# A diffusion step on one core: descriptor memory doubled, y tiles in the shared buffers, two dot tiles moved into the first network

## The chip, the core and the metric

The kernel runs on one core of one Trainium2 chip. The core has TensorE (PE in the profile; PEld is its weight load), VectorE (DVE), ScalarE (ACT), GpSimd (POOL) and SyncE (SP). POOL and SP issue DMA transfers, each on a queue of its own, and 16 DMA engines move the bytes for both. The metric is the time of one execution in microseconds of device time; lower is better.

## The reference

One step of a diffusion backbone with two layers, on 512 latent tokens and 128 context tokens, with 1024 features. Every sub-layer has the same frame: the input is normalised and modulated by a shift and a scale, goes through the sub-layer, and is added back to the residual with a gate.

```
m = silu(cvec) @ mod_w[i] + mod_b[i]          # six vectors of 1024 per layer and condition
h = rmsnorm(x, g) * (1 + scale) + shift
x = x + gate * mixer(h)                       # layer 0: SSD scan; layer 1: differential attention
x = x + gate2 * conv_ffn(h2)                  # h2: x normalised and modulated again

def conv_ffn(h, up_w, conv_w, conv_b, down_w):
    u = dwconv(h @ up_w, conv_w, conv_b)      # 1024 -> 2 x 2816, width 3 along the tokens
    a, v = jnp.split(u, 2, axis=-1)
    return (jax.nn.silu(a) * v) @ down_w      # 2816 -> 1024
```

The layer-0 modulation is needed at once. That of layer 1, a 6144 x 1024 matrix times two conditioning vectors, is needed only from attention on, so the kernel computes it bit by bit beside other work. These are the "dots".

## The kernel before

Features lie on the 128 partitions and the 640 tokens along the free axis, so a residual is eight tiles `x` of 128 x 640. Every matmul is made of three: operands are split into a high and a low part of a rounded format, and hi*hi, hi*lo and lo*hi are added up. Weights come through `raw` buffers by SP (`prefetch`, line 166); `cast` makes the high part on ACT (`whi`, line 103) and the low part (`wlo`) on DVE. For part of the up weights (`self.summed`) the low part is made without DVE: ACT writes minus the high part into `wlo`, and POOL issues a transfer that reads the weights from memory again and adds them to it (line 204). POOL does such accumulating transfers in two more places: the low part of the network's middle tiles (`ml<-cv`, line 724), and the sum of a down projection (`xd<-y`, line 357).

A network (`ffn`) runs over 22 pairs of hidden tiles. In the first network the first six pairs are plain products; from then on `pair8` does the pair with seven products of sums of quarter matrices, made on DVE (tiles `s`). `SUB` cuts the pairs at 4, 8, 12 and 16. After each cut (one pair into the next part) `project_out` multiplies the middle tiles by their part of the down weights, for eight output tiles: ACT scales each by its gate into a tile `y`, and POOL adds y to the residual, which lies in memory as `xd` during the network. The fifth part adds into the residual in SBUF after `restore` has loaded it.

The dots are the generator `mod_rest`. For each of 48 tiles it loads 128 x 1024 weights into one of two `mw` buffers (SP, line 667) and makes two reductions on DVE (line 674), one for each condition. `DOTS = 3, 34, 48` says where: tiles 0 to 2 before the first network, 3 to 33 in it, 34 to 47 in attention. A hook that TensorE's loops call counts steps ("ticks"); between two reductions the generator waits `self.gap` of them. In the first network a plain pair has 16 ticks and the gap is 3; a seven-product pair has 14 and the gap 10; a projection of eight tiles has 32, with a gap of 4 in the first and 5 in the next three. In attention the gap is 6. What is left of the dots is drained after the last pair of the network, and in attention before the output projection; only then is the memory of the weights and conditions given back and the residual reloaded.

Buffers have tags. `t` has 4 buffers (line of `tmp`), `f` has `NF = 11`, for raw up products (`uraw`), sums `s`, and others. In the first network the even y lie in `t`, the odd ones in a tag `y` with 2 buffers of the network's own pool; in the second all eight lie in `y` with 3. Two of the last three norm tiles that are made while the first network starts (`late`) lie in `y` as well, the third in `f`. The order of each engine's instructions is set by the planner of the framework from the program's order and its own estimate of when operands come free; a few are given high priority. POOL issues in order: a transfer that waits holds all behind it.

The program reserves `dynamic_dma_scratch_size` bytes of every partition, at address 0 of SBUF, for the descriptors of the transfers that POOL issues.

Of the kernel before, what the change touches and what calls it, by code (L numbers as in the profile page):

```python
# [40 lines left out]
RAW = 4  # L41
NS = 4
S0 = 6, 4
DOTS = 3, 34, 48
TH = T // 2
ATT_SPLIT = 6
NF = 11
# [3 lines left out]
class Step:  # L51
# [643 lines left out]
    def ffn(self, l, h, nextnorm, pool):  # L695
        nc = self.nc
# [46 lines left out]
        def operands(out, tp):  # L743

            B = [[[tuple(cut(t, j) for t in h[ns * k + i]) for i in range(ns)] for j in range(2)] for k in range(2)]
            Ts = [[], [], [], []]
            late = []
            for i in range(ns):
                f1, f2 = self.tmp("f1"), self.tmp("f2")
                for f, k in ((f1, i), (f2, ns + i)):  # L750
                    self.tt(f, h[k][0].bitcast(F32), h[k][1].bitcast(F32), ALU.add)
                    yield 1
                t12, t43 = self.slot("f", "t12", bufs=NF), self.slot("f", "t43", bufs=NF)
                self.tt(cut(t12, 0), cut(f1, 1), cut(f1, 0), ALU.subtract)
                self.tt(cut(t12, 1), cut(f2, 1), cut(t12, 0), ALU.subtract)
                self.tt(cut(t43, 0), cut(f2, 0), cut(t12, 1), ALU.subtract)
                self.tt(cut(t43, 1), cut(f2, 1), cut(f1, 1), ALU.subtract)
                yield 2
                hi, lo = (tp.tile([P, 3 * TH], F32R, tag=f"T{nm}{i}", name=f"T{nm}{i}", bufs=1) for nm in "hl")
                x4 = tuple(cut(t, 1) for t in h[i])  # L760
                late.append((x4, cut(t43, 0)))
                parts = (slice(0, T), t12), (slice(T, T + TH), cut(t43, 1))
                for o, x in parts:
                    self.act(hi[:, o], x, AF.Copy)
                    self.tt(lo[:, o], x, hi[:, o].bitcast(F32), ALU.subtract)
                    yield 1
                for j in range(3):
                    Ts[j].append((cut(hi, j), cut(lo, j)))
                Ts[3].append(x4)
                yield 2  # L770
            rest = [[tuple(cut(t, j) for t in h[k]) for k in range(2 * ns, KT)] for j in range(2)]
            out.extend((B, Ts, rest, late))
# [58 lines left out]
        def pair(p, more):  # L831
            if p >= S0[l]:
                if p == S0[l]:
                    self.drain(self.seven)
                    finish_operands()
                return pair8(p, more)
            ua = copy_out(self.next_tile(h, "up"))
            epilogue(p, ua, copy_out(self.next_tile(h, "up")))

        self.start_tiles(h)  # L840
        done = 0
# [6 lines left out]
        with self.tc.tile_pool(name=f"sums{l}", bufs=1, side="right", reuse_waits="tile") as tp:  # L848
            self.seven = self.add(operands(sevens, tp), 1)
            for s, (k0, k1) in enumerate(SUB):  # L850
                while done < min(k1 + 1, FT):
                    if not l and done == 3:
                        junk = lambda: self.slot("sq", "junk", BF16, cols=1024, bufs=1)
                        self.modtask = self.add(self.mod_rest(1, *DOTS[:2], self.cb, self.mod_row, junk), 1)
                    self.gap, self.rest = 3 if done < S0[0] else 10, 0
                    pair(done, done + 1 < min(k1 + 1, FT))
                    done += 1
                if s < len(SUB) - 1:
                    self.gap = 5 if s else 4
                    if self.modtask:  # L860
                        self.modtask[1] = self.ticks + 1
                    self.project_out(mid, range(k0, k1), self.gate(l, 1),
                                     to=lambda i: self.slot("y", "y", bufs=3 if l else 2, pool=pool) if l or i % 2
                                     else self.tmp("y"))
        if self.modtask:
            self.drain(self.modtask)
            self.modtask = None
# [271 lines left out]
    def ssd(self, h, dtps, nextnorm, pool):  # L1139
# [62 lines left out]
        self.gap, self.rest = 4, 3  # L1202
        early = self.add(self.mod_rest(1, 0, DOTS[0], self.cond_rows(row), row, junk), 8)
        self.project_last(hy, range(8), self.gate(0, 0), nextnorm, save=True, before=[early])
# [201 lines left out]
    def heads(self, h, nextnorm, pool):  # L1406
# [9 lines left out]
        self.gap, self.rest = 6, 0  # L1416
        dots = self.add(self.mod_rest(1, *DOTS[1:], self.cb, self.mod_row, junk), 10)
        for hd in range(8):
# [38 lines left out]
    def weight_units(self):  # L1457
# [9 lines left out]
        def ffn(l):  # L1467
# [13 lines left out]
            return out  # L1481

        u = [(*x, None, None) for x in u] + ffn(0)
        v, u = u, []
        for hd in range(8):
# [5 lines left out]
              for i in range(0, KT - 3, per) for j in (min(i + per, KT - 3),)]  # L1491
        u += [(a["w_ao"][i], D) for i in range(KT - 3, KT)]
        return v + [(*x, None, None) for x in u] + ffn(1)

    def run(self):
        tc, nc, a = self.tc, self.nc, self.a
        self.units = self.weight_units()
        name = lambda u: self.units[u][0] is not None and self.units[u][0].name
        up = [u for u in range(len(self.units)) if name(u) == a["w_up"].name]
        after = {u for u in up if name(u - 1) and name(u - 1) != a["w_up"].name}  # L1500
        half = len(up) // 2
        self.summed = (set(up) - set(up[:5]) - set(up[half:half + 5]) - after)
        self.x = []

        def norm(l, s, h):
            def mk(hf):
                if hf == "A":
                    h.extend(self.new_h(f"h{l}{s}"))
                return self.norm_task(hf, self.gs[l][s], self.shift(l, s), h)
            return mk  # L1510

        hs = [[] for _ in range(4)]
        psd = lambda: tc.tile_pool(name="psd", bufs=3, space=PSUM, reuse_waits="tile")
        psb = lambda: tc.tile_pool(name="psb", bufs=6, space=PSUM, reuse_waits="tile")
        self.open_x()
        scond = ExitStack()
        sp = scond.enter_context(tc.tile_pool(name="scond", bufs=1, reuse_waits="tile"))
        with psd() as self.psd:
            with tc.tile_pool(name="first", bufs=1, reuse_waits="tile") as pool, tc.manual_schedule():
                self.silu_cond(sp)  # L1520
                dtps = self.first_tiles(hs[0], pool)
            with (tc.tile_pool(name="sconst", bufs=1, reuse_waits="tile") as cp,
                  tc.tile_pool(name="ssd", bufs=1, reuse_waits="tile") as pool):
                self.ssd_consts(cp)
                self.ssd(hs[0], dtps, norm(0, 1, hs[1]), pool)
        scond.close()
        with psb() as self.psb, tc.tile_pool(name="ffn0", bufs=1, reuse_waits="tile") as pool:
            self.px = pool
            y = lambda: self.slot("y", "nty", bufs=2, pool=pool)
            self.late = [y, y, lambda: self.slot("f", "ntl", bufs=NF)]  # L1530
            self.ffn(0, hs[1], norm(1, 0, hs[2]), pool)
            self.px = None
        self.psb = None
        self.deep = 1
        with psd() as self.psd:
            self.attention(hs[2], norm(1, 1, hs[3]))
        with psb() as self.psb, tc.tile_pool(name="ffn1", bufs=1, reuse_waits="tile") as pool:
            self.px = pool
            self.ffn(1, hs[3], self.final_task, pool)
            for t in reversed(list(self.tasks)):  # L1540
                self.drain(t)
        self.xctx.close()
# [99 lines left out]
```

## Time and profile before

| | us |
|---|---|
| median of three runs (lowest, highest) | 1868.93 (1862.59, 1873.59) |
| the profiled execution's own time | 1865.18 |
| its span, first to last instruction | 1863.4 |
| first SSD mixer and what stands ahead | 0 to 566 |
| first network | 566 to 1050 |
| attention and its output projection | 1050 to 1400 |
| second network and final norm | 1400 to 1863 |

Rows of the timeline give the start, the time taken, engine, line, operation, output and inputs, and in brackets how long the engine had been idle and what the profile names as the end of that idle time. Rows of waits give the total, the number and the longest. Rows by stage give for each engine the busy time and the number of instructions, then the granted clock of TensorE, the share of the 16 DMA engines that was busy, and GB/s. A busy share above 1 comes from packets that overlap. A wait is named after the releaser that the profile can see; where POOL waits inside its own descriptor code, the name can be of an unrelated instruction.

### The profile page before, as it was taken

Reading aid. Unit: us, or ns where it says so; the run is one execution under the profiler, and the core shown is the slowest. Engines: PE = TensorE matmul, PEld = TensorE weight load, DVE = VectorE, ACT = ScalarE, POOL = GpSimd, SP = SyncE. Lnnn points to the kernel's source line nnn. Section 1 sums busy time; section 2 is a strip of 40 time slices with the busy share of each in tenths; the row PEclk is TensorE's granted clock in tenths of the full one; section 3 lists DMA queues with packets and bytes.
Section 4 is the critical chain, followed back from the end, with each engine's and each line's share of the span. In section 5 each row is a group of like instructions: output and inputs, shape, how many; then the busy total and the mean of one; then the engine's idle time right before and its main releaser. Section 6 shows DMA issues by size and latency. Waiting matters only on the chain. (4 is left out here: it accounts for less than half of the span.)

```text
span 1863.4 us, 33793 instructions
## 1 busy us (share of the span) xinstructions
PE 1786.0 (96%) x12914; PEld 1687.5 (91%) x12914; DVE 1463.6 (79%) x2907; ACT 1169.8 (63%) x2329; POOL 154.4 (8%) x180
## 2 busy tenths in 40 slices
PE   7999999999999989899989989999999999999997
PEld 5899999999899989898989988888889999999996
DVE  6699999999768867778776788888968856758584
ACT  3489687878337555676564555666636766767661
POOL 0000000000001111221210000000000121222210
PEclk9999999999999999999999999999999999999998
DMA  9835344446647686877866222222334588787871
GB/s 341 275 113 150 96 148 107 138 134 205 205 158 178 179 232 161 199 196 184 225 151 217 86 85 80 82 87 80 102 126 110 113 171 175 155 183 152 175 194 57
DMA packets 116990, 289.13 MB, mean 155 GB/s; under 512 B 13422, under 2 KB 20186, under 8 KB 116828
## 3 DMA queue, kind: packets, MB, share of 16 engines
q1 hardware_dynamic: 90908, 223.92, 36.9%
q0 software_dynamic: 25344, 62.53, 19.8%
q8 instruction: 101, 1.65, 0.4%
q10 hardware_dynamic: 576, 0.52, 0.1%
q14 instruction: 61, 0.50, 0.1%
HBM read 238.36 MB, written 34.80 MB: 147 GB/s over the span
## 5 line engine op out<-in xcount | busy, mean ns | idle before, releaser
L103 ACT ACTIVATE whi<-raw 128x1024 fp32r<-128x1024 f32 (+2 forms) x259 | 226.2, 873 | 183.2 <-PE po L112 110.6
L109 DVE TENSOR_TENSOR wlo<-raw,whi 128x1024 fp32r<-128x1024 f32 (+3 forms) x188 | 188.4, 1006 | 41.1 <-ACT whi L103 40.5
L112 PE MATMUL po<-ml,whi 128*128 128x256 f32 (+1 forms) x704 | 165.8, 309 | 2.4 <-DMA ml<-cv 2.4
L204 POOL DMA_DIRECT2D wlo<-in_w_up x70 | 62.1, 887 | 1254.9 <-DVE ca L106 590.7
L112 PE MATMUL po<-mh,whi 128*128 128x256 f32 (+1 forms) x704 | 165.7, 309 | 0.2 <-ACT mh L103 0.2
L112 PE MATMUL po<-mh,wlo 128*128 128x256 f32 (+1 forms) x704 | 165.3, 309 | 0.0
L109 DVE TENSOR_TENSOR wlo<-s,whi 128x512 fp32r<-128x512 f32 x136 | 92.0, 688 | 60.6 <-ACT whi L103 60.2
L112 PE MATMUL up<-h01h,wlo 128*128 128x320 f32 (+2 forms) x400 | 114.6, 316 | 18.2 <-DMA wlo<-in_w_up 18.2
L103 ACT ACTIVATE whi<-s 128x512 fp32r<-128x512 f32 x136 | 84.4, 629 | 74.9 <-DVE s L109 55.9
L112 PE MATMUL up<-Th,whi 128*128 128x320 f32 x408 | 127.9, 313 | 3.1 <-ACT uraw L103 3.1
L112 PEld LDWEIGHTS po<-ml,whi 128*128 128x128 f32 x704 | 127.7, 188 | 3.2 <-DMA ml<-cv 3.2
L112 PEld LDWEIGHTS po<-mh,whi 128*128 128x128 f32 x704 | 127.6, 188 | 0.7 <-ACT mh L103 0.4
L112 PEld LDWEIGHTS po<-mh,wlo 128*128 128x128 f32 x704 | 127.9, 188 | 0.1
L112 PE MATMUL up<-Th,wlo 128*128 128x320 f32 x408 | 127.4, 312 | 0.0
L112 PE MATMUL up<-Tl,whi 128*128 128x320 f32 x408 | 127.3, 312 | 0.0
L106 DVE SCALAR_TENSOR_TENSOR cv<-uraw,fcw,cv 128x511 f32<-128x511 f32 (+1 forms) x176 | 85.7, 547 | 37.5 <-ACT cv L103 37.4
L112 PE MATMUL up<-h01l,whi 128*128 128x320 f32 (+2 forms) x400 | 113.3, 313 | 0.0
L112 PE MATMUL up<-h01h,whi 128*128 128x320 f32 (+2 forms) x400 | 113.3, 313 | 0.0
L112 PE MATMUL up<-h11h,wlo 128*128 128x320 f32 (+1 forms) x368 | 107.3, 309 | 3.0 <-DMA wlo<-in_w_up 3.0
L112 PE MATMUL up<-h11l,whi 128*128 128x320 f32 (+1 forms) x368 | 107.0, 308 | 0.0
L112 PE MATMUL up<-h11h,whi 128*128 128x320 f32 (+1 forms) x368 | 107.0, 308 | 0.0
L106 DVE SCALAR_TENSOR_TENSOR ca<-uraw,fcw,ca 128x511 f32<-128x511 f32 (+1 forms) x176 | 86.8, 547 | 10.0 <-ACT ca L103 8.1
(531 smaller groups left out, 5387.2 us busy)
## 6 DMA issues: line engine op xcount, KB each, us to landing
raw<-in_w_up SPq DMA_DIRECT2D x88, 512.0 KB, 4.1
mw<-in_modT SPq DMA_DIRECT2D x45, 512.0 KB, 6.9
raw<-in_w_in SPq DMA_DIRECT2D x40, 512.0 KB, 6.0
rb<-rowd SPq DMA_DIRECT2D x40, 512.0 KB, 5.7
xd<-y POOLq DMA_DIRECT2D x64, 320.0 KB, 7.2
wlo<-in_w_up POOLq DMA_DIRECT2D x36, 512.0 KB, 6.5
raw<-in_w_dn SPq DMA_DIRECT2D x64, 256.0 KB, 2.9
ml<-cv POOLq DMA_DIRECT2D x42, 320.0 KB, 4.1
```

Source lines behind the costliest of these rows:

```text
L103: return self.nc.scalar.activation(out, in_, func, **k)
L106: return self.nc.vector.scalar_tensor_tensor(out, in0, s, in1, op0, op1)
L109: return self.nc.vector.tensor_tensor(out, a, b, op)
L112: self.last = self.nc.tensor.matmul(out, lhsT, rhs, start=start, stop=stop, skip_group_check=more)
L204: self.nc.gpsimd.dma_start(lo[:, c], self.units[u][0][:, c], accum_op=ALU.add)
```

## The change

Three things in one. The descriptor memory goes from 1024 to 2048 bytes of a partition. The tag `y` goes from the first network: odd y and the late norm tiles use `f`, and the second network keeps its three `y` buffers. Tiles 34 and 35 of the dots go from attention into the first network, where the gap falls from 10 to 9 ticks in seven-product pairs and from 5 to 4 in the second to fourth projection. No arithmetic changes.

```diff
-DOTS = 3, 34, 48
+DOTS = 3, 36, 48
...
-                    self.gap, self.rest = 3 if done < S0[0] else 10, 0
+                    self.gap, self.rest = 3 if done < S0[0] else 9, 0
...
-                    self.gap = 5 if s else 4
+                    self.gap = 4
...
-                                     to=lambda i: self.slot("y", "y", bufs=3 if l else 2, pool=pool) if l or i % 2
-                                     else self.tmp("y"))
+                                     to=lambda i: self.slot("y", "y", bufs=3, pool=pool) if l
+                                     else self.slot("f", "y", bufs=NF) if i % 2 else self.tmp("y"))
...
-            y = lambda: self.slot("y", "nty", bufs=2, pool=pool)
-            self.late = [y, y, lambda: self.slot("f", "ntl", bufs=NF)]
+            self.late = [lambda: self.slot("f", "ntl", bufs=NF)] * 3
...
-    nc = bacc.Bacc("TRN2", target_bir_lowering=False, num_devices=1, dynamic_dma_scratch_size=1024)
+    nc = bacc.Bacc("TRN2", target_bir_lowering=False, num_devices=1, dynamic_dma_scratch_size=2048)
```

## The prediction

> **What bounds the kernel now.** Read the head of the page, then the busy times by stage, then what TensorE waits for in the stage that idles most, and only then the queues behind that wait.
>
> ```profile
> span 1863.4 us, 33793 instructions
> PE 1786.0 (96%) x12914; PEld 1687.5 (91%) x12914; DVE 1463.6 (79%) x2907; ACT 1169.8 (63%) x2329; POOL 154.4 (8%) x180
> ```
>
> TensorE is busy 1786.0 of 1863.4 us, and the change alters no matmul. All it can win or lose is idle time of PE, 77 us, and time at a lower clock. Busy times of the first network from its seven-product pairs on, of attention and of the second network:
>
> ```profile
> 680.00:1000.00 320.00, 297.07 (x1956) 294.06 (x1955) 243.40 (x446) 201.51 (x367) 58.64 (x67) 0.97 0.77 190
> 1060.00:1330.00 270.00, 254.50 (x1775) 225.05 (x1773) 235.73 (x481) 166.87 (x351) 0.00 (x0) 0.99 0.26 82
> 1440.00:1800.00 360.00, 357.04 (x2435) 356.10 (x2435) 244.73 (x439) 249.54 (x458) 74.42 (x85) 1.00 0.75 162
> ```
>
> After the length come PE, weight loads, DVE, ACT and POOL busy, the granted clock, the DMA share and GB/s. PE idles 22.9 us in the first network, 15.5 in attention, 3.0 in the second network, which does the same work without dots. What it waits for from 570 to 1000 us, then each large wait (idle time in brackets):
>
> ```profile
> PE up L112 <- DMA wlo<-in_w_up: 18.2, 6, 6.5
> PE up L112 <- ACT uraw L103: 3.1, 1, 3.1
> PE po L112 <- DMA ml<-cv: 2.4, 3, 1.0
> ...
> 675.48 0.41 PE L112 MATMUL up<-h01h,wlo 128*128 128x320 f32 x1 [0.81 <-DMA wlo<-in_w_up]
> 697.10 0.41 PE L112 MATMUL up<-h01h,wlo 128*128 128x320 f32 x1 [1.82 <-DMA wlo<-in_w_up]
> 769.07 0.42 PE L112 MATMUL up<-h01h,wlo 128*128 128x320 f32 x1 [4.82 <-DMA wlo<-in_w_up]
> 849.03 0.41 PE L112 MATMUL up<-h01h,wlo 128*128 128x320 f32 x1 [2.25 <-DMA wlo<-in_w_up]
> 853.10 0.42 PE L112 MATMUL up<-h01h,wlo 128*128 128x320 f32 x1 [2.06 <-DMA wlo<-in_w_up]
> 936.78 0.64 PE L112 MATMUL up<-h01h,wlo 128*128 128x320 f32 x1 [6.46 <-DMA wlo<-in_w_up]
> ```
>
> The waits from 769 on stand where a down projection (eight accumulating `xd<-y`) hands over to the next pair, whose low weights come by an accumulating transfer on the same POOL queue; so does the one at 675. The single wait on `uraw` (3.1) and the one at 697 follow the first projection, whose pace of dots stays as it is. After some of them the clock is granted at half:
>
> ```profile
> 760.00:780.00 20.00, 15.18 (x93) 14.92 (x93) 12.01 (x23) 10.39 (x17) 2.98 (x4) 0.91 0.76 176
> 930.00:950.00 20.00, 13.54 (x83) 13.28 (x82) 9.75 (x19) 9.90 (x17) 2.62 (x3) 0.83 0.58 137
> ```
>
> A clock of 0.91 and 0.83 over 20 us costs (1 - 0.91) x 20 = 1.8 and 3.4 us on top of the idle time.
>
> **The descriptor memory.** POOL's issues around the stall at 769, ACT's two producers, one landing (the transfer issued at 749.43 takes 7.9 us):
>
> ```profile
> 749.43 0.88 POOL L357 DMA_DIRECT2D xd<-y  x1 [1.04 <-DVE wlo L109]
> 750.38 0.88 POOL L204 DMA_DIRECT2D wlo<-in_w_up  x1
> 751.98 0.86 POOL L357 DMA_DIRECT2D xd<-y  x1 [0.72 <-ACT y L103]
> 757.62 0.89 POOL L357 DMA_DIRECT2D xd<-y  x1 [4.78 <-ACT uraw L103]
> 761.46 0.89 POOL L204 DMA_DIRECT2D wlo<-in_w_up  x1 [2.95 <-DVE uraw L109]
> ...
> 752.37 1.14 ACT L103 ACTIVATE y<-po,mod 128x256 f32<-128x256 f32 x3
> 753.34 0.70 ACT L103 ACTIVATE wlo<-raw 128x512 fp32r<-128x512 f32 x1
> ...
> xd<-y POOLq DMA_DIRECT2D x1, 320.0 KB, 7.9
> ...
> DMA to landing us min/median/max: 4.2/7.2/12.0
> DMA to landing us min/median/max: 4.5/6.3/12.2
> ```
>
> The last two rows are the landings of all 64 xd<-y and of all 70 wlo.
>
> The y of the issue at 757.62 was ready at 752.37 + 1.14 = 753.51, yet POOL sat idle. The named ACT release is not its producer. It went 0.3 us after the landing at 749.43 + 7.9 = 757.3, the third transfer before it. So three transfers fill the memory, and a fourth waits for the first. The wlo for which PE stalls was ready at 753.34 + 0.70 = 754.04 and went at 761.46, some 7 us late. With twice the memory six or more fit (estimate, in proportion) and this wait goes.
>
> What is late next decides. POOL issues in order, so the same transfers stay ahead of that wlo. The question is whether the DMA engines ever ran dry while POOL was held:
>
> ```profile
> q0 software_dynamic: 463, 1.23, 63.8%
> q1 hardware_dynamic: 434, 1.57, 42.0%
> ...
> q0 software_dynamic: 331, 1.03, 105.8%
> q1 hardware_dynamic: 11, 0.02, 1.4%
> ```
>
> Packets, MB and share of 16 engines of the queue fed by POOL (q0) and of SP's (q1), first from 755 to 765, then from 672 to 677. In the first stretch the engines are full: 63.8 + 42.0 = 106%, and q0 moves 1.23 MB in 10 us. In the second, again with no more than three transfers under way, q0 alone fills them and moves 1.03 MB in 5 us. Three transfers are enough to keep the engines busy, so issuing a fourth sooner only lengthens the line. The wlo lands when the bytes ahead of it are through. I take 0.5 us for each of the four late-issued stalls (0.81, 4.82, 2.06, 6.46), the two ends of a line where some engines have finished before the slowest: **-2 us**. Ends: +1 (SP's loads get less of full engines), and, if the landing followed the issue, all four waits and both clock losses, 14.15 + 5.2 = -19.3.
>
> The Trainium skill ("DMA: Bandwidth & Descriptors", on queues, rings and completion order) says that each engine takes turns between the queues it has work for, packet by packet. By that a longer q0 earns no larger part, and the two stretches agree: q0 moves 0.12 MB per us beside q1 and 0.21 alone. Its figure for the time of one such transfer says otherwise; it stands with the first rival.
>
> **The dots and their pace.** Each tile is one 512 KB load and two DVE reductions:
>
> ```profile
> L674 DVE CUSTOM_DVE_ANT_0 junk<-mw,cb x45: 1202/1220/1227, 612.7 to 1328.4; 128x1024 bf16<-128x1024 f32 x45
> L674 DVE CUSTOM_DVE_ANT_0 mw<-mw,cb x45: 1214/1222/1228, 615.4 to 1330.3; 128x1024 f32<-128x1024 f32 x45
> ...
> 722.00:770.00 48.00, 42.15 (x287) 41.63 (x287) 33.65 (x57) 27.20 (x55) 11.40 (x13) 0.99 0.92 229
> 811.00:855.00 44.00, 39.70 (x268) 39.12 (x267) 30.21 (x53) 24.28 (x50) 10.50 (x12) 1.00 0.92 235
> 860.00:895.00 35.00, 34.50 (x235) 34.24 (x234) 32.78 (x63) 25.76 (x44) 5.23 (x6) 1.00 0.67 149
> ```
>
> Two more tiles in the first network are 2 x 2 x 1.22 = 4.9 us of DVE and 1 MB through SP's queue, behind which weight loads stand. The steps between dots fall from 5 to 4 in three projections of 32 ticks: 32/10 = 3.2 tiles become 32/8 = 4, so 0.8 more loads in each, where the engines are at 0.92 of their time (last rows, second to last column). A pair of 14 ticks goes from 14/20 = 0.70 to 14/18 = 0.78 tiles: 0.08 x 2.44 = 0.2 us of DVE per pair, where DVE is busy 32.78 of 35 us. That fits into the 2.2 us left; without that cover the eleven pairs that carry dots cost 2.2. The two tiles more are made up for by 3 x 0.8 and the pairs, so the dots end no later than now, before the drain that follows the last pair; were they left to that drain, each would put 2.4 us of DVE in front of the reload of the residual. Price of a load in front of a critical wlo: 0.512 MB at the rate of both queues in the first stretch, (1.23 + 1.57)/10 = 0.28 MB per us, so 1.8 us. Nearest row for no cost is the 860 to 895 stretch, with loads and hardly a stall. The quicker pace brings loads forward as well, ahead of the handover, so I take half for one load: **+1 us**; ends -2 (a load less at a handover) and 3 x 1.8 + 2.2 = +7.6.
>
> In attention two tiles go from the end. PE's waits from 1295 to 1345 us:
>
> ```profile
> PE po L112 <- ACT e L103: 1.0, 2, 0.8
> PE sl L112 <- ACT v L103: 0.6, 1, 0.6
> PE wpt L1358 <- DVE rs_v L240: 0.4, 1, 0.4
> PE vt L1245 <- DVE wTl L109: 0.3, 1, 0.3
> ```
>
> They sum to 2.3 us. The last dots (1328.4, 1330.3) sit in front of the last head's chain there, and the residual's reload waits for their memory. The early heads keep their dots at the old pace. I take **-2 us**; ends -4 (with 1.7 of a changed rhythm) and 0.
>
> **The tiles.** Odd y move from two buffers of their own to the eleven general ones, three norm tiles likewise, and no instruction is added; all tiles lie 1 KB higher, and the planner that orders each engine's instructions may choose another order, which I can't price. Four more claims fall between two uses of a slot; the next taker of the last y is a pair later, over 12 us, against a landing of 12.0 us at most: 0, between -1 and +2.
>
> **Sum.** -2 + 1 - 2 + 0 = -3 us on the profiled execution's own 1865.18 us, that is 1862. This execution lies 3.75 us under the median of the runs shown, 1868.93, so the median comes to **1866 us**. Under 0.5%, 9.3 us, this kernel's measurement hardly tells from no change, so the forecast is: same. With the ends half reached (memory -3 to +0.5, pace -1 to +4, attention -3 to -1, tiles -0.5 to +1) its own range is 1868.9 - 7.5 to + 4.5, or 1861 to 1873.
>
> **The rivals.**
> Faster: the landing follows the issue. For it: the wlo waited 7 us for memory and PE waited 4.82 for the wlo; the second network, where POOL is rarely held, idles 3.0 us. Against: full engines while it waited. It gives 1868.9 - 19.3 = 1850. The Trainium skill, on the same page in its section on the anatomy of a DMA by the software path, speaks for this one: it fits 2.0 us plus bytes/436e3, by which (an estimate) a 512 KB transfer sent at once would land after 3.2 us, long before PE comes. The rows differ: no wlo landed under 4.5 us, and the slowest took 12.2.
> Slower: the quicker dots put their loads in front of the critical wlo. For it: the stage with loads stalls 18.2 us on wlo, the one without 3.0. Against: quicker dots also bring their loads forward, away from the handover. It decides once each of three handovers has one load more: 5.4 us, and a half-clock stretch each like that of 1.8 us, 5.4 more: 1868.9 + 10.8 = 1880.
> Nothing happens: the limit of three is not the descriptor memory's. For it: nothing on the page names it. Against: the issue 0.3 us after a landing. POOL's gaps stay, and only pace and attention count: 1868.
>
> **Chances.** Forecast 0.50, nothing happens 0.05, both within 0.5%; faster rival 0.25; slower rival 0.20. So faster 0.25, same 0.55, slower 0.20. The range reaches to both rivals, 1846 to 1880.
>
> **What would show it.** Right: POOL issues each xd<-y within half a microsecond of its y; transfers take longer to land; PE's waits on wlo stay, within a few us of 18.2; dots end before 930 and, in attention, by 1300. Wrong: those waits fall under 5 us with the second network's pattern, or the clock of the first network drops below 0.97.

## The result and the profile after

| | before | after |
|---|---|---|
| median, us (lowest to highest, 4 executions each, on one chip) | 1871.26 (1862.59 to 1875.11) | 1850.46 (1847.69 to 1852.4) |
| ratio to before, with its 95% interval | | 0.9894 [0.9854, 0.9934] |
| the profiled execution's own time, us | 1865.18 | 1847.69 |

The kernel became faster by about 1.1%. A second measurement of the same program, beside the experiments below, gave 0.9946 [0.9926, 0.9965], with a median of 1856.73 us. The two intervals overlap only from 0.9926 to 0.9934, so the gain lies somewhere between 0.4% and 1.5%. The forecast of 1866 lies 16 us above the first median. That median is the "faster" rival's number, 1850. Whether it came by that rival's mechanism is what the experiments have to say.

The head of the page after and the three stages (same columns as before):

```profile
span 1845.9 us, 33794 instructions
PE 1782.4 (97%) x12914; PEld 1684.1 (91%) x12914; DVE 1465.1 (79%) x2907; ACT 1166.3 (63%) x2329; POOL 153.4 (8%) x180
...
680.00:1000.00 320.00, 305.66 (x2036) 302.81 (x2035) 256.52 (x469) 206.64 (x376) 58.28 (x67) 0.98 0.80 202
1050.00:1320.00 270.00, 255.36 (x1793) 225.56 (x1793) 237.16 (x485) 167.47 (x353) 0.00 (x0) 0.99 0.26 84
1425.00:1785.00 360.00, 358.48 (x2446) 357.82 (x2445) 245.93 (x441) 250.02 (x461) 73.96 (x85) 1.00 0.75 163
```

The first network changed: PE idles 14.3 us in its 320 us window, where it idled 22.9. The other two windows stand as they were. Where each stage begins can be read off the short matmuls `st` that open every sub-layer's norm. Below are those of the first network (`h01h`), of attention (`h10h`) and of the second network (`h11h`); the last times in each row are the first and last start. First before, then after:

```profile
L112 PE MATMUL st<-h01h,whi x48: 276/332/386, 559.4 to 582.3; 128*128 128x256 f32 x24, 128*128 128x384 f32 x24
L112 PE MATMUL st<-h10h,whi x48: 276/334/582, 1038.1 to 1061.5; 128*128 128x256 f32 x24, 128*128 128x384 f32 x24
L112 PE MATMUL st<-h11h,whi x48: 276/333/386, 1406.4 to 1428.9; 128*128 128x256 f32 x24, 128*128 128x384 f32 x24
```

```profile
L112 PE MATMUL st<-h01h,whi x48: 276/332/385, 561.0 to 584.1; 128*128 128x256 f32 x24, 128*128 128x384 f32 x24
L112 PE MATMUL st<-h10h,whi x48: 276/334/579, 1027.6 to 1050.7; 128*128 128x256 f32 x24, 128*128 128x384 f32 x24
L112 PE MATMUL st<-h11h,whi x48: 276/333/386, 1391.7 to 1414.1; 128*128 128x256 f32 x24, 128*128 128x384 f32 x24
```

The first network went from 1038.1 - 559.4 = 478.7 to 466.6 us, attention from 368.3 to 364.1. So of the 17.5 us between the two spans, 12.1 lie in the first network and 4.2 in attention. The first network's gain shows in what TensorE waits for from 570 to 1000 us, in the profile after:

```profile
PE up L112 <- DMA wlo<-in_w_up: 8.2, 6, 3.7
```

The waits on `wlo` fell from 18.2 to 8.2 us, and the longest from 6.5 to 3.7. The clock adds its part: summed over the clock records, 10.2 us were lost to a lowered clock in the first network before, 5.5 after. So 10.0 us of waits and 4.7 of clock make up the 12.1 (2.6 came back elsewhere). The prediction had named the place and the wait. What it had not foreseen was that they would halve.

### The profile page after: what moved, and what is told of

Its sections match the earlier page's. It is cut to its first block, busy times and chain, and to the rows that moved or that the text cites. A ratio compares the mean times of both kernels' runs of the same rounds, so it can differ in the third digit from the quotient of the medians.

```text
span 1845.9 us, 33794 instructions
## 1 busy us (share of the span) xinstructions
PE 1782.4 (97%) x12914; PEld 1684.1 (91%) x12914; DVE 1465.1 (79%) x2907; ACT 1166.3 (63%) x2329; POOL 153.4 (8%) x180
## 3 DMA queue, kind: packets, MB, share of 16 engines
q0 software_dynamic: 25344, 62.53, 19.9%
## 4 chain that ended last, share of the span: by engine, by line
PE 41%; DVE 9%; issue 7%; DMA 4%; ACT 2%; POOL 1%; DVEq 0%; POOLq 0%; ACTq 0%
PE up L112 15%; PE po L112 15%; DMA wlo<-in_w_up 3%; PE k L112 2%; PE st L112 2%; PE q L112 2%; DMA ml<-cv 1%; PE ov L112 1%; PE sl L112 1%; PE v L112 1%; ACT e L103 1%; PE wt L1375 1%; DVE sm L1309 1%; DVE wlo L109 1%; DVE w L106 1%
```

## The experiments

Three theories were set against each other. **Memory:** with room for more transfers each issue goes at once, and the low weights land sooner. **Order:** the descriptor memory does nothing, and the gain comes from the tiles in other buffers, which give the planner another order of work. **Pace:** it comes from when the dots issue their loads. This table holds what all kernels measured; the text under each experiment adds to it. Lengths of stages are those of one profiled execution, from the `st` rows as above; the wait is the total of TensorE's waits on `wlo` from 570 to 1000 us. The last column is the length of attention less what the clock records show as lost there.

| kernel | median, us | ratio to before [95%] | first network | wait on wlo | attention less clock loss |
|---|---|---|---|---|---|
| before (profile) | | | 478.7 | 18.2 | 363.3 |
| after (profile) | 1850.46 | 0.9894 [0.9854, 0.9934] | 466.6 | 8.2 | 361.0 |
| e4: after again | 1856.73 | 0.9946 [0.9926, 0.9965] | 470.2 | 9.0 | 360.2 |
| e1: after, 1024 bytes | 1856.48 | 0.9958 [0.9938, 0.9978] | 470.8 | 8.2 | 360.1 |
| e2: tiles alone | 1860.07 | 0.9972 [0.9951, 0.9993] | 470.7 | 10.8 | 362.9 |
| e3: tiles and memory | 1861.5 | 0.9975 [0.9954, 0.9997] | 473.8 | 13.2 | 363.7 |
| e5: dots and pace alone | 1855.96 | 0.9942 [0.9923, 0.9960] | 470.3 | 2.2 | 360.2 |
| e6: after, 34 tiles | 1859.76 | 0.9957 [0.9933, 0.9981] | 470.0 | 7.3 | 362.0 |
| e7: after, 512 bytes | 2072.06 | 1.1097 [1.1067, 1.1127] | 586.5 | 75.3 | |
| e8: no loads of dots | 1848.58 | 0.9895 [0.9869, 0.9921] | 454.0 | 5.0 | |
| e9: gap 4 alone | 1854.27 | 0.9940 [0.9921, 0.9959] | 464.4 | 5.4 | 362.9 |
| e10: gap 9 alone | 1850.04 | 0.9917 [0.9894, 0.9940] | 461.4 | 3.8 | 363.8 |
| e11: dots kept off the handover | 1850.96 | 0.9930 [0.9907, 0.9953] | 465.1 | 6.2 | 360.3 |
| e12: after, 39 tiles | 1860.21 | 0.9972 [0.9951, 0.9992] | 473.0 | 11.5 | 362.9 |

Two executions of one program (after and e4) differ by 3.6 us in the first network and by 2.3 us in attention as it stands, so single stages are no finer than that. Kernels e1 to e4 share one chip and its runs of before (median 1864.91), e5 to e8 a second group (1866.65), e9 to e12 a third (1865.94).

### After with the old descriptor memory (e1), beside after again (e4)

```diff
-    nc = bacc.Bacc("TRN2", target_bir_lowering=False, num_devices=1, dynamic_dma_scratch_size=2048)
+    nc = bacc.Bacc("TRN2", target_bir_lowering=False, num_devices=1, dynamic_dma_scratch_size=1024)
```

Every engine has the same instructions in the same order in both, so these two differ by the memory alone.

> The changed kernel with 1024 bytes of descriptor memory again; every engine's instructions stand in the same order as in the changed kernel, so only the memory differs. If the engines were full and the descriptor memory gives nothing (the prediction), it keeps the gain: ratio to before 0.988 to 0.992, about 1851 us, although POOL again waits for the third transfer before. If the landing follows the issue, it loses the first network's and the second's part of the gain, 12 us or more: ratio 0.996 to 1.003, 1862 to 1875 us.

> The changed kernel again, on the same chip as e1 to e3: ratio 0.986 to 0.993, so that the four runs form a square of descriptor memory by pace. If memory and pace add up, e4 - e1 equals e3 - e2 within 3 us; if they need each other, it is the larger by 5 us or more.

The medians are 1856.48 and 1856.73 us, the ratios to before 0.9958 and 0.9946, each within +-0.002. The means of the two differ by 0.8 us, with an uncertainty of about 3 us, so no worth of the larger memory is shown, and one of 2 us couldn't be seen. Both ratios missed what was expected of them (0.988 to 0.992 and 0.986 to 0.993), because the gain itself is smaller in these runs than in the first measurement. If the landing followed the issue, e1 should be 12 us slower or more; it isn't. The timelines say why. POOL's issues at the second handover, after (2048 bytes), then the landing of the last of them (its last number, in us from its issue) and the first matmul that uses it:

```profile
749.07 0.88 POOL L204 DMA_DIRECT2D wlo<-in_w_up  x1 [0.74 <-PE po L112]
750.16 0.86 POOL L357 DMA_DIRECT2D xd<-y  x1 [0.21 <-issue]
753.54 0.89 POOL L357 DMA_DIRECT2D xd<-y  x1 [2.52 <-ACT y L103]
755.95 0.89 POOL L204 DMA_DIRECT2D wlo<-in_w_up  x1 [1.52 <-PE up L112]
...
wlo<-in_w_up POOLq DMA_DIRECT2D x1, 256.0 KB, 9.5
...
765.46 0.41 PE L112 MATMUL up<-h01h,wlo 128*128 128x320 f32 x1 [0.62 <-DMA wlo<-in_w_up]
```

The same instructions with 1024 bytes (e1), with the landings of the transfers issued at 747.42, 754.85 and 762.59:

```profile
747.42 0.86 POOL L357 DMA_DIRECT2D xd<-y  x1 [4.62 <-issue]
750.30 0.89 POOL L357 DMA_DIRECT2D xd<-y  x1 [2.01 <-issue]
753.25 0.88 POOL L357 DMA_DIRECT2D xd<-y  x1 [2.06 <-ACT whi L103]
754.85 0.87 POOL L204 DMA_DIRECT2D wlo<-in_w_up  x1 [0.73 <-PE po L112]
757.53 0.86 POOL L357 DMA_DIRECT2D xd<-y  x1 [1.81 <-issue]
760.12 0.89 POOL L357 DMA_DIRECT2D xd<-y  x1 [1.72 <-ACT uraw L103]
762.59 0.88 POOL L204 DMA_DIRECT2D wlo<-in_w_up  x1 [1.59 <-DVE s L109]
...
xd<-y POOLq DMA_DIRECT2D x1, 320.0 KB, 7.1
...
wlo<-in_w_up POOLq DMA_DIRECT2D x1, 512.0 KB, 7.4
...
wlo<-in_w_up POOLq DMA_DIRECT2D x1, 256.0 KB, 8.1
...
770.75 0.41 PE L112 MATMUL up<-h01h,wlo 128*128 128x320 f32 x1 [0.61 <-DMA wlo<-in_w_up]
```

With 1024 bytes the limit of three is plain: 747.42 + 7.1 = 754.5, and the third issue after it goes at 754.85; 754.85 + 7.4 = 762.25, and the third after that goes at 762.59. With 2048 bytes it is gone: the wlo of 755.95 goes while the wlo of 749.07, third before it, is still under way (it landed 8.1 us after its issue, at 757.2). Set both by the last scaling of a `y`, which starts at 752.09 in after and at 757.39 in e1. The critical wlo is issued 3.9 us behind it with the larger memory and 5.2 us with the smaller, yet lands 13.4 and 13.3 us behind it, and TensorE waits 0.62 and 0.61 us. Issued 1.3 us sooner, it landed at the same moment.

The first handover is the clearer case, as there the larger memory brings the issue forward most. The issue of that handover's second `wlo`, after and then in e1:

```profile
661.63 0.87 POOL L204 DMA_DIRECT2D wlo<-in_w_up  x1
...
668.88 0.90 POOL L204 DMA_DIRECT2D wlo<-in_w_up  x1 [3.53 <-issue]
```

Counted from the start of the projection's last matmul, it is issued 0.1 us ahead of it in after and 6.3 us behind it in e1, and lands 14.9 and 15.3 us behind it (15.0 and 9.0 us from its issue). At the three later handovers the landings of after and e4 lie between 1.4 us before and 1.6 us behind those of e1. So here a sooner issue did not bring a sooner landing. The engines were full while POOL was held: in e1 an issue stands 0.3 us behind the landing of the third transfer before it in 24 places, and over the 47 us for which POOL stood idle before them the 16 engines' busy share is 1.06 (before: 20 places, some 48 us, 1.05).

### The tiles alone (e2), and with the memory (e3)

```diff
-                                     to=lambda i: self.slot("y", "y", bufs=3 if l else 2, pool=pool) if l or i % 2
-                                     else self.tmp("y"))
+                                     to=lambda i: self.slot("y", "y", bufs=3, pool=pool) if l
+                                     else self.slot("f", "y", bufs=NF) if i % 2 else self.tmp("y"))
...
-            self.late = [y, y, lambda: self.slot("f", "ntl", bufs=NF)]
+            self.late = [lambda: self.slot("f", "ntl", bufs=NF)] * 3
```

That is e2, on the kernel before; e3 has 2048 bytes as well. The larger memory without these tiles doesn't fit into SBUF: the `y` buffers pay for it. It could not be tried alone.

> Before, with the y and late norm tiles in the general buffers alone. Prediction: nothing, 0.999 to 1.001 (1868 to 1872 us). If the two y buffers held ACT back, ratio 0.995 or less and the y of each projection come evenly.

> Before, with the general buffers and 2048 bytes, and the dots and their pace as before (the doubled memory does not fit without the freed y buffers). Prediction: 1 to 2 us under e2. If the landing follows the issue: 12 to 19 us under e2, ratio 0.990 to 0.994, with waits on wlo under 6 us in the first network. If the gain needs the quicker pace: no more than 5 us under e2.

The tiles alone (`y` and the late norm tiles in the general buffers) give 0.9972 [0.9951, 0.9993], some 5 us; the memory on top gives 0.9975, so again nothing is shown (the means of e2 and e3 agree to 0.1 us, with an uncertainty of about 3). The tiles, put at 0, do count, and no instruction was added or removed for it. What changed is the order on ACT. In the kernel before, from the second projection's fourth `y` to its seventh (casts of the next weights left out):

```profile
737.57 1.10 ACT L103 ACTIVATE y<-po,mod 128x256 f32<-128x256 f32 x3 [1.94 <-PE po L112]
743.86 1.30 ACT L103 ACTIVATE whi<-s 128x512 fp32r<-128x512 f32 x2 [5.19 <-DVE s L109]
...
746.02 1.08 ACT L103 ACTIVATE y<-po,mod 128x256 f32<-128x256 f32 x3
747.93 1.10 ACT L103 ACTIVATE y<-po,mod 128x256 f32<-128x256 f32 x3
750.36 1.12 ACT L103 ACTIVATE y<-po,mod 128x256 f32<-128x256 f32 x3
```

And in e2, the fourth to the last:

```profile
738.11 1.10 ACT L103 ACTIVATE y<-po,mod 128x256 f32<-128x256 f32 x3 [1.94 <-PE po L112]
...
742.52 1.08 ACT L103 ACTIVATE y<-po,mod 128x256 f32<-128x256 f32 x3
...
747.27 1.08 ACT L103 ACTIVATE y<-po,mod 128x256 f32<-128x256 f32 x3
...
750.23 1.10 ACT L103 ACTIVATE y<-po,mod 128x256 f32<-128x256 f32 x3
752.03 1.10 ACT L103 ACTIVATE y<-po,mod 128x256 f32<-128x256 f32 x3 [0.70 <-PE po L112]
```

Before, ACT stands 5.19 us in front of `whi<-s`, a cast that waits for DVE's sum of the next pair's weights, and the next four `y` are queued behind it. The fourth to the fifth `y` takes 746.02 - 737.57 = 8.45 us, and then they follow at about 2 us, so the last transfers bunch at the handover. In e2 the planner put that cast behind the sixth `y`, where it waits for nothing, and they come every 1.8 to 4.8 us (after: 2.7 to 4.4). The moment that counts for TensorE is the landing of the second wlo at each of the three handovers behind the later projections, counted from the start of the projection's last matmul: 17.7, 17.5 and 17.8 us before; 14.8, 15.3 and 17.1 in e2; 13.5, 14.6 and 14.9 after. TensorE needs it at about 13 us.

That the order is the cause is not shown by a run: it was never changed alone. The last handover speaks against it as the whole cause. There the `y` come as evenly in e2 (every 3.5 to 4.4 us, where before the fifth stood 8.7 us behind the fourth), yet the wlo lands only 0.7 us sooner, and TensorE waits 5.96 us for it instead of 6.46.

### The dots alone (e5), and after with the old split (e6)

```diff
-DOTS = 3, 34, 48
+DOTS = 3, 36, 48
...
-                    self.gap, self.rest = 3 if done < S0[0] else 10, 0
+                    self.gap, self.rest = 3 if done < S0[0] else 9, 0
...
-                    self.gap = 5 if s else 4
+                    self.gap = 4
```

That is e5, on the kernel before. e6 is after with `DOTS = 3, 34, 48`.

> Before, with the dots and their pace of the change alone: y in its two buffers, 1024 bytes. If y's buffers (through the order in which ACT gets its work) and the pace each give their part and add up, 0.9986 +- 0.002, and the fifth y of the second projection stays late by 4 us as before. If the pace alone does it, 0.996 or less, and waits on wlo of 8 to 9 us. If the quicker pace without the buffers puts loads in front of the handover (the slower rival), 1.002 or more.

> The changed kernel with tiles 34 and 35 of the dots in attention again, all else (buffers, memory, gaps of 9 and 4 ticks) as changed. The prediction put 2 us on the two tiles in attention: the stage from attention to the second network then takes 2 us more than in the changed kernel, the first network the same or up to 2 us less; ratio 0.995 to 0.997. If attention gains 4 us, as the one profile of the changed kernel has it, 0.997 to 0.999.

The dots alone give 0.9942 [0.9923, 0.9960], 11 us, with old tiles and old memory, and the wait on wlo goes nearly whole:

```profile
PE up L112 <- DMA wlo<-in_w_up: 2.2, 2, 2.0
```

Yet the first network is 470.3 us long here, no shorter than with the tiles alone (10.8 us of waits): the lowered clock still takes 10.8 us of it, and TensorE's other waits add up to 16. The old order of `y` that was expected to stay did not: at the second projection the fifth `y` follows the fourth by 3.9 us, at the fourth projection by 10.1, more than before. So the pace of the dots moves ACT's order too. As to the split, in e6 it is the only difference from e4; 0.9957 against 0.9946, in two groups of runs, tells nothing. Attention tells more. Less the clock loss it takes 362.0 to 363.8 us in six kernels with 34 tiles (before, e2, e3, e6, e9, e10; mean 363.1) and 360.1 to 361.0 in five with 36 (after, e1, e4, e5, e11; mean 360.4), so the two tiles are worth about 2.7 us there. TensorE's idle time in attention, which needs no correction for the clock, agrees: 19.9 to 20.2 us in the six, 17.6 or 17.7 in the five.

### One step of pace at a time (e9, e10)

```diff
-                    self.gap = 5 if s else 4
+                    self.gap = 4
```

is all of e9, and

```diff
-                    self.gap, self.rest = 3 if done < S0[0] else 10, 0
+                    self.gap, self.rest = 3 if done < S0[0] else 9, 0
```

all of e10, both on the kernel before.

> Before, with the gap of 4 instead of 5 ticks in the second to fourth projection and nothing else. If the quicker dots of the projections bring their last loads forward, away from the handover, this carries most of e5's gain: ratio 0.994 to 0.997, waits on wlo in the first network under 6 us. If it needs the gap of 9 or the two moved tiles, 0.998 or more.

> Before, with the gap of 9 instead of 10 ticks in the seven-product pairs and nothing else. If the projections' gap does it, 0.998 to 1.002 and waits on wlo of 12 us or more. If before is an unlucky arrangement that nearly any shift of the loads breaks, 0.994 to 0.997 here too.

Each alone is faster than before: 0.9940 and 0.9917, 11 and 15 us, with 34 tiles, 1024 bytes and the old buffers. So a gain of this size needs neither the memory, nor the `y` in other buffers, nor the two moved tiles of dots. Were the gains independent, both together would give 0.9940 x 0.9917 = 0.9858; e5, which has both and the two tiles, gives 0.9942 [0.9923, 0.9960]. So they don't add up. Nor do the tiles add to the pace: e1, which has the tiles, the dots and the pace with the old memory, measures 0.9958, no better than e5 without the tiles. The account that fits is that each moves the kernel off an arrangement in which the handover went badly, and that once off it there is little more to win. The landings, counted as above, agree with it: 13.9, 12.5 and 12.6 us in e9, 13.5, 12.5 and 12.7 in e10, against 17.5 to 17.8 before. Who shares the DMA engines there, by queue (packets, MB, share of 16 engines), in the 5 us from the start of the second projection's last matmul, before, after and e10:

```profile
q0 software_dynamic: 166, 0.42, 45.7%
q1 hardware_dynamic: 189, 0.71, 45.0%
```

```profile
q0 software_dynamic: 342, 0.99, 102.3%
q1 hardware_dynamic: 32, 0.11, 5.8%
```

```profile
q0 software_dynamic: 217, 0.67, 69.9%
q1 hardware_dynamic: 161, 0.59, 35.8%
```

Before, SP's loads take as large a share as the accumulating transfers, which move 0.42 MB; after, POOL's queue has the engines nearly to itself and moves 0.99; e10 lies between. By SP's issues in the timelines, before sent loads of dots 1.3 us ahead of that matmul's end and 4.8 us behind it, and loads of weights 2.4 us ahead and 2.4 us behind; after sent the dots 4.7 us ahead and 2.2 us behind, and the weights 0.9 and 3.4 us behind. On ACT the block ahead of `whi<-s` is still there in e9 and e10 at this handover. In e9 the long step (6.3 us, not 8.4) still leads to the fifth `y`; in e10 it (7.3 us) leads to the fourth, so that more of the last `y` come at their even pace again.

### Without the loads (e8), and with dots kept off the handover (e11)

```diff
+        first = t0 == DOTS[0]
+        kept = []
...
-                nxt = alloc()
-                nc.sync.dma_start(nxt, a["modT"][t + 1])
+                if first and len(kept) == 2:
+                    nxt = kept[t % 2]
+                else:
+                    nxt = alloc()
+                    nc.sync.dma_start(nxt, a["modT"][t + 1])
+                    kept.append(nxt)
...
-                i = nc.vector.tensor_tensor_reduce(w if c else junk, w, cb[c], 1.0, 0.0, ALU.mult, ALU.add,
+                i = nc.vector.tensor_tensor_reduce(w if c and not first else junk, w, cb[c], 1.0, 0.0, ALU.mult, ALU.add,
```

e8, on the kernel before, leaves out 29 of the 31 loads of dots in the first network; the reductions run on the two tiles that are there, so layer 1's modulation is not computed. e11, on after, quickens the dots and then lets none go in the last three tiles of a projection and in the pair behind it:

```diff
-                    self.gap, self.rest = 3 if done < S0[0] else 9, 0
+                    self.gap, self.rest = 3 if done < S0[0] else 7, 0
...
-                    self.gap = 4
+                    self.gap = 3 if s else 4
...
+                    def pause(i, y):
+                        if s and i == 4 and self.modtask:
+                            self.modtask[1] = self.ticks + 26
+                        return y
...
-                                     to=lambda i: self.slot("y", "y", bufs=3, pool=pool) if l
-                                     else self.slot("f", "y", bufs=NF) if i % 2 else self.tmp("y"))
+                                     to=lambda i: pause(i, self.slot("y", "y", bufs=3, pool=pool) if l
+                                     else self.slot("f", "y", bufs=NF) if i % 2 else self.tmp("y")))
```

> Before, with 29 of the 31 loads of dots in the first network left out: the reductions run on the two tiles loaded first, both into the junk tile, so layer 1's modulation is not computed. If the bytes ahead of wlo make PE wait (the prediction), the waits on wlo in the first network fall from 18.2 to under 6 us although POOL still waits for the third transfer before, and the run is 10 to 20 us shorter: ratio 0.989 to 0.995. If the descriptor memory makes it wait whatever the bytes, they stay above 12 us and the ratio above 0.997.

> The changed kernel with no dots in the last three tiles of the second to fourth projection and in the pair behind each; to make up, the gap is 3 ticks in the rest of these projections and 7 in the pairs. If loads beside the handover make PE wait for wlo, the waits in the first network fall from 8 or 9 us to under 5, and the kernel is 3 to 6 us faster than the changed one: ratio 0.991 to 0.994. If the dots that DVE does more in the pairs cost as much, or the weights' own loads make it wait, 0.994 to 0.997.

e8 gives 0.9895 [0.9869, 0.9921]: all traffic of the dots' loads costs some 20 us, which bounds what their timing can win in the first network. Its stage, in the columns of before:

```profile
680.00:1000.00 320.00, 311.97 (x2128) 309.82 (x2127) 255.08 (x467) 209.22 (x382) 58.52 (x67) 1.00 0.73 175
```

PE idles 8.0 us of 320 instead of 22.9, at full clock, with DVE busier than before (255.08 against 243.40 us) and POOL's memory as small. So DVE's time isn't what the dots cost here; their loads are. A load has two sides, its bytes in the engines and its place in SP's queue, where SP stands waiting for a dot's reduction before a load of dots in 25 places (102.6 us from 570 to 1000 us in before) with the weights behind it. e8 takes away both and can't tell them apart. At the handover at 769 it was not SP's queue: the critical wlo was ready 7 us before it was sent.

e11 gives 0.9930 [0.9907, 0.9953], inside the band expected if the loads beside the handover were the cause (0.991 to 0.994), but with 6.2 us of waits on wlo, where under 5 were expected. It is not told apart from after (0.9894 and 0.9946), so no gain of a hard exclusion on top of the pace is shown.

### Half the old memory (e7)

```diff
-    nc = bacc.Bacc("TRN2", target_bir_lowering=False, num_devices=1, dynamic_dma_scratch_size=2048)
+    nc = bacc.Bacc("TRN2", target_bir_lowering=False, num_devices=1, dynamic_dma_scratch_size=512)
```

> The changed kernel with 512 bytes, a quarter, in the same order of instructions. In proportion it holds one transfer, or at most two halves of one. If a few transfers under way are what keeps the engines full, this starves the queue: each of some 170 transfers waits for the landing of the one before it, 4 to 5 us alone, and in the projections, with 9 transfers in 29 us, the line grows: 15 us or more slower than 1024 bytes, ratio 1.004 or more. If the depth matters in no way, 0.993 to 0.997.

2072.06 us, ratio 1.1097 [1.1067, 1.1127], more than 200 us, where 15 or more had been expected. The memory does matter, on its other side. The stage, TensorE's waits from 570 to 1000 us, some of POOL's issues, and the landings of the first three:

```profile
680.00:1000.00 320.00, 241.97 (x1539) 238.41 (x1539) 198.98 (x364) 154.21 (x288) 48.41 (x56) 0.87 0.67 156
...
PE up L112 <- DMA wlo<-in_w_up: 75.3, 10, 15.8
...
734.10 0.88 POOL L204 DMA_DIRECT2D wlo<-in_w_up  x1 [5.99 <-issue]
739.53 0.88 POOL L204 DMA_DIRECT2D wlo<-in_w_up  x1 [4.55 <-ACT ca L103]
745.68 0.87 POOL L724 DMA_DIRECT2D ml<-cv  x1 [5.28 <-ACT ml L103]
749.86 0.88 POOL L204 DMA_DIRECT2D wlo<-in_w_up  x1 [3.30 <-ACT p L103]
...
wlo<-in_w_up POOLq DMA_DIRECT2D x1, 512.0 KB, 5.1
...
wlo<-in_w_up POOLq DMA_DIRECT2D x1, 256.0 KB, 4.0
...
ml<-cv POOLq DMA_DIRECT2D x1, 320.0 KB, 3.9
```

734.10 + 5.1 = 739.2, and the next goes at 739.53; 745.68 + 3.9 = 749.6, and the next goes at 749.86. One transfer is under way at a time, in all 176 issues of the run. With one, POOL's queue starves TensorE, which idles 78 of the 320 us; with three (e1) it idles 16.7; beyond three no gain is shown. Three was enough already; two was not run.

### Five tiles moved (e12)

```diff
-DOTS = 3, 36, 48
+DOTS = 3, 39, 48
```

> The changed kernel with five tiles of dots moved into the first network instead of two, at the same gaps, so that they fall into the pairs after the fourth projection. If each tile out of attention is worth 1.2 us, as two were 2.5 in the profiles, three more give 3 to 4 us and the first network loses 1 or 2: ratio 0.992 to 0.995. If they only fill what the last pairs have left and attention's end is bound by its last head, no gain: 0.995 to 0.998.

0.9972 [0.9951, 0.9992], with 11.5 us of waits on wlo. Three tiles more than after gain nothing: the first network is 473.0 us long, and attention less its clock loss is at 362.9, longer than with two tiles moved. TensorE idles 18.8 us in attention, against 17.6 with two tiles moved and about 20 with none, so the three gave back half of what the two had won. Why is not shown. So the 2.7 us are not a price for each tile.

## Why the prediction was right and wrong

**The descriptor memory, -2 us: right in its mechanism; the 2 us are not shown.** e4 less e1 is -0.8 us and e3 less e2 is 0.0, by means, each with an uncertainty of about 3 us. No run shows the 0.5 us that the sum took for each of four stalls. The reading that three transfers already fill the engines, and that a sooner issue only lengthens the line, is what e1 and after show: 1.3 us sooner issued at one handover and 6.4 at another, the wlo landed within 0.4 us of the same moment. The expected signs came: with 2048 bytes an `xd<-y` goes within half a microsecond of its `y`, and the slowest landings grew to 14.8 us (`xd`, e4) and 15.5 (`wlo`), from 12.0 and 12.2.

**The faster rival: right number, wrong mechanism.** It said that the landing follows the issue. It doesn't, and e1 has nearly the same gain with the old memory. That its 1850 came is chance: the same program's second median is 1856.73, and the gain came by the parts that the sum had put at 0 and +1, with the 2 us of attention.

**The tiles, 0 between -1 and +2: wrong.** They measure about -5 us (0.9972 [0.9951, 0.9993]). The step that failed is the one that said the planner "may choose another order, which I can't price" and then took 0. Buffers were costed as claims on slots; what came with them was another order of ACT's work, and that this order made the gain is argued, not shown. A row that bears on it stood in the trace of before: ACT idle for 5.19 us in front of a cast, with four `y` behind it.

**The dots' pace, +1 between -2 and +7.6: wrong in sign.** It measures -11 us (e5, some 2.7 of it in attention), and -11 and -15 for its two halves alone. The slower rival, which rested on the same step, is refuted with it. The term priced the loads by their number (0.8 more in each projection). The sentence that the quicker pace "brings loads forward as well, ahead of the handover" was in the direction of the runs, but it was allowed only to halve a cost. With two more loads in the first network the kernel got faster, so at these paces their number is not what decides. What the rows by queue suggest instead, and no run changed alone, is which bytes lie in front of the critical wlo in the few microseconds of the handover. What those waits cost stood in the same profile: 14.15 us of waits at four handovers plus the clock loss behind them. e8 later put the whole of the loads at 20 us.

**Attention, -2: right** in size (about 2.7 us), with its signs: the last dots of attention are at 1281.5 us, by 1300, and the last of the first network start before 910, by 930. Its reason, that the last dots sit in front of the last head's chain, fits two tiles but not five, which give less (e12).

**The sum.** The change measured -8 us (e4, 1856.73 - 1864.91) and -20.8 (the first measurement, by medians), where the sum had -3. So a gain that can be told from none was missed, and the low median lies inside the stated 1846 to 1880 because that range was stretched to both rivals, not because the sum had it. The parts measured alone, memory 0 to -1, tiles -5 and dots with their pace -11, would make -16 or -17. The two halves of the pace don't add up, and e1 against e5 shows nothing of the tiles once the pace has changed, so a sum of terms was the wrong form for them: they seem to cure one stall. Of the signs, "PE's waits on wlo stay, within a few us of 18.2" was wrong (8.2).

**What stays open.** Whether the order of ACT's work or the moment of SP's loads decides the landing at the handover: between the kernels compared here both moved at once, and neither was changed alone. In e9 and e10 the block on ACT stayed and only its place or length moved, and in e2 an even order left the last handover's wait at 5.96 us; both speak against a cure that needs no more than an even order. Whether e10 or e11 is better than after: their ratios (0.9917 and 0.9930) are lower than e4's 0.9946 but not than after's first 0.9894, and the intervals overlap.

## What to carry to other kernels

When an issue is held by a full descriptor memory, ask first whether the engines behind it ever ran dry: here three transfers kept them full, and room for more moved the issue and not the landing. A stall at a handover that depends on which of several transfers are ahead is a property of the arrangement; one tick of pace, or another buffer for a tile, was worth 0.3 to 0.8% here, and two such edits needn't add up, so measure such edits one by one before putting any down to the part of the change that looks largest. Don't put an edit that changes only buffers at zero: here it changed the order of an in-order engine, which had stood 5 us in front of a waiting instruction.

## What the runs showed of the hardware

The number of POOL's transfers under way goes in steps with the descriptor memory: one with 512 bytes, three with 1024, up to six seen with 2048. From 512 to 1024 it isn't in proportion to the bytes, and with 2048, in after and e4, no issue was seen to wait for a landing. The transfers carry 256 to 512 KB. A refused issue leaves no record of its own: POOL shows idle time put down to an unrelated instruction (`ACT ca`, `ACT ml`, `DVE s`) or to "issue", and the issue stands about 0.3 us behind a landing.

Sent with no other of POOL's under way, as in e7, such a transfer lands slowly too: all wlo of that run took

```profile
DMA to landing us min/median/max: 3.6/5.1/8.4
```

The Trainium skill ("DMA: Bandwidth & Descriptors", on the anatomy of a DMA by the software path) has a fit of 2.0 us plus bytes/436e3, by which 512 KB take 3.2 us and 256 KB 2.6 (an estimate). The rows do not agree: 5.1 for the 512 KB and 4.0 for the 256 KB transfer above, with no other transfer of POOL under way, though SP's moved 0.27 MB beside the first and 0.02 MB beside the second. The measurement decides, and no transfer of this kind landed by the fit.
